# SBUF pools of a float32 decoder layer, regrouped by the engine that reads them: TensorE's operands at the low bytes of each partition, the rest at the high bytes

## The chip, the cores and the metric

The kernel runs on one core of a Trainium2 chip. The metric is the device time of one launch in microseconds; a run of the kernel is timed as a whole, and one further execution is profiled. TensorE (PE in the profile) multiplies, VectorE (DVE) and ScalarE (ACT) do everything elementwise, SyncE (SP) issues nearly all transfers from HBM into SBUF, the on-chip memory of 128 partitions. A tile takes the same bytes of every partition, so its place is one number: its first byte within a partition.

## The reference

One decoder layer over 256 tokens of width 2048, all in float32. What matters here is that nearly all of it is matrix products of the same 256 tokens with large weights, each weight used once:

```python
x = layer_norm(ALPHA * x + 0.5 * swiglu(x, ffn1_w_in[i], ffn1_w_out[i]), ...)   # D_FF = 5504
z = x @ mix_w_in[i]                                                              # 2048 x 11264
... short conv and gated linear recurrence on parts of z ...
merged = sigmoid(gate_conv) * (y_conv @ branch_w_conv[i]) + sigmoid(gate_hgrn) * (y_hgrn @ branch_w_hgrn[i])
x = layer_norm(ALPHA * x + merged @ mix_w_out[i], ...)
x = layer_norm(ALPHA * x + 0.5 * swiglu(x, ffn2_w_in[i], ffn2_w_out[i]), ...)
ple = sigmoid(x @ ple_w_gate[i]) * (p[i] @ ple_w_proj[i])
x = layer_norm(ALPHA * x + ple, ...)
```

## The kernel before

**Products.** Each float32 product is done as three float32r products (lines 733 to 735): weight and activation are each split into a rounded half and a remainder (`wh`, `wl` for the weight; `xh`, `xl`, or `gh`, `gl`, or `mh`, `ml`, or `ph`, `pl` for the activation), and `wh` times `xh`, `wl` times `xh`, `wh` times `xl` are accumulated into one PSUM tile `acc`. The activation half, 128 by 128, is the stationary operand that LDWEIGHTS loads (PEld in the profile); the weight half, 128 partitions by 512 columns (2,048 bytes of each partition), is the moving operand that MATMUL streams. So every MATMUL has a LDWEIGHTS of its own, and while one MATMUL streams its moving operand from SBUF, the LDWEIGHTS of the next reads its stationary operand from SBUF.

**Work.** A `Unit` is 256 tokens (two token tiles, t = 0 and 1) times a slab of a weight, at most 512 columns wide. A weight comes in pieces of two k-tiles: one DMA of 512 KB into a tile `raw` (four of them), one ScalarE cast to `wh` (line 679), one VectorE subtraction to `wl` (line 681), and then 2 k-tiles x 3 products for t = 0 and again for t = 1: 12 MATMULs for each piece. The units follow each other in phases: `ffn1`, `hgrn` (the projection `mix_w_in` with conv and recurrence in the background), `merge` (the gates and branch products, then `mix_w_out`), `ffn2`, `ple`.

**Where the halves lie.** `wh` and `wl` have six buffers each in the pool `wp` ("main"). The pool `region` is closed and opened again for every phase, with whatever tiles the phase needs, and what is free there holds some more `wh` and `wl` buffers: EXTRA says how many, and the plan deals the pieces out in that proportion, so in `ffn1` 4 of 10 pieces lie in the region, in `ffn2` 3 of 9, in `ple` 1 of 7, in `hgrn` and `merge` none:

```python
NMAIN = 6
EXTRA = {"ffn1": 4, "hgrn": 0, "merge": 0, "ffn2": 3, "ple": 1}
plan.append((u, ks, kind if (i + 1) * n // (NMAIN + n) > i * n // (NMAIN + n) else "main"))
```

The activation halves `xh`, `xl`, `gh`, `gl` lie in the pool `op`; in `merge`, half of the merged activation's halves (`mh`, `ml`, the last two of four column chunks) lie in the region; `ph` and `pl`, the stationary operands of the four products with `ple_w_proj`, lie among the constants.

**What orders the work.** The order within each engine comes from the program text and a scheduler; SBUF is filled by pools from one end, in the order in which they are opened: `const`, `res` (the residual `x`), `wp` (`raw`, `wh`, `wl`), `op`, `st` (small and intermediate tiles), and the region last. The built program uses nearly all of the 224 KiB of a partition.

Of the kernel before, what the change touches and what calls it, by code (L numbers as in the profile page):

```python
# [10 lines left out]
F32 = mybir.dt.float32  # L11
F32R = mybir.dt.float32r
# [5 lines left out]
P = 128  # L18
# [5 lines left out]
CC = 512  # L24
KG = 2
# [10 lines left out]


class Stat:
    """A stationary operand, transposed (contraction on partitions), as the two
    float32r halves of its float32 values; four k-tiles of one token tile per SBUF tile."""  # L40

    def __init__(self):
        self.parts = {}
# [4 lines left out]


class Unit:  # L50
    """256 tokens times a [nk * 128, width] slab of a weight."""

    def __init__(self, stat, w, row, nk, col, width, epi, split=SPLIT):
        self.stat, self.w, self.row, self.nk = stat, w, row, nk
# [11 lines left out]
def hybrid_layer(ctx: ExitStack, tc: tile.TileContext, x, p, ln_g, ln_b, ffn1_w_in, ffn1_w_out, mix_w_in,  # L66
# [4 lines left out]
    def pool(name, bufs=1, **kw):  # L71
        return ctx.enter_context(tc.tile_pool(name=name, bufs=bufs, **kw))

    const = pool("const")
    res = pool("res")
    wp = pool("wp")
    op = pool("op")
    st = pool("st")
    region = {}

    def open_region(kind):
        """The one SBUF region whose contents change from phase to phase."""
        if "ctx" in region:
            region.pop("ctx").close()
        region["ctx"] = ExitStack()
        region["kind"] = kind
        region["pool"] = region["ctx"].enter_context(tc.tile_pool(name=kind, bufs=1, reuse_waits="tile"))

    def rtile(shape, dtype=F32, **kw):
        return region["pool"].tile(shape, dtype, **kw)  # L90
# [2 lines left out]
    ps_t = pool("ps_t", 2, space=PSUM)  # L93
    ps_h = pool("ps_h", 2, space=PSUM)

    # ---------------------------------------------------------------- scheduling helpers
    state = {"tick": 0}
    later = []
    unsettled = set()
# [34 lines left out]
        return stat.get(t, k)  # L134

    def gated(part):
        """Queue the next instructions of a kind behind the one set down in gate."""
        ins, n = gate.get(part, (None, 0))
        gate[part] = (ins, n - 1)
        return tc.issue_after(ins) if n > 0 else nullcontext()  # L140

    def settle(c):
        """Force what is still to be done in place on column chunk c of x."""
        while c in unsettled:
            later.pop(0)[1]()

    # ---------------------------------------------------------------- constants, small inputs
    ident = const.tile([P, P], F32, name="ident")
    make_identity(nc, ident)
    ones = const.tile([P, 1], F32, name="ones")  # L150
    nc.gpsimd.memset(ones, 1.0)
    xt = [res.tile([P, D], F32, tag=f"x{t}", name=f"x{t}") for t in range(NT)]
    xin = x[0].rearrange("(t p) d -> t p d", p=P)
# [15 lines left out]
                                pattern=[[2 * b, n], [0, b]], channel_multiplier=-1)  # L169
        masks[b] = m  # L170

    # ---------------------------------------------------------------- operand transposition
    def transposed(src, nb):
        tp = ps_t.tile([P, CC], F32, tag="tp", name="tp")
        for i in range(nb):
# [1 line left out]
        return tp  # L177

    def halves(stat, t, g, src, nb, tag):
        """hi (rounded to float32r) and lo = src - hi (exact in float32r)."""  # L180
        where, bufs = (region["pool"], 4) if tag == "m" else (op, 8)
        h = where.tile([P, 4, P], F32R, tag=tag + "h", name=tag + "h", bufs=bufs)
        l = where.tile([P, 4, P], F32R, tag=tag + "l", name=tag + "l", bufs=bufs)
        hf = h[:, :nb, :].rearrange("p a b -> p (a b)")
        lf = l[:, :nb, :].rearrange("p a b -> p (a b)")
        nc.scalar.copy(hf, src)  # L186
        nc.vector.tensor_tensor(out=lf, in0=src, in1=hf.bitcast(F32), op=ALU.subtract)  # L187
        stat.parts[t, g] = (h, l)
# [3 lines left out]
        halves(stat, t, g, tp[:, : nb * P], nb, tag)  # L192

    def turn_blocks(dst, src, nb):
        """dst[:, a, :] = transpose of the a-th 128 columns of src, 32 by 32 on the vector engine."""
        cols = src[:, : nb * P].rearrange("p (a b c) -> p a b c", b=4, c=32)
        for q in range(4):
            for b in range(4):
                nc.vector.transpose(dst[32 * b : 32 * b + 32, :nb, 32 * q : 32 * q + 32], cols[32 * q : 32 * q + 32, :, b, :])  # L199
# [3 lines left out]
        turn_blocks(y, src, nb)  # L203
        halves(stat, t, g, y[:, :nb, :].rearrange("p a b -> p (a b)"), nb, tag)

    # ---------------------------------------------------------------- layer norm
    stats = {}

    def ln_stat(t, c):
# [2 lines left out]
        nc.vector.bn_stats(stats[t][:, c, :], xt[t][:, c * CC : (c + 1) * CC])  # L212

    def rsqrt_of(v, n, mul, add):
        """1 / sqrt(v * mul + add), one Newton step after the engines' sqrt and reciprocal."""
        w = st.tile([P, n], F32, tag=f"w{n}", name="w", bufs=4)
        m = st.tile([P, n], F32, tag=f"n{n}", name="m", bufs=4)
        r = st.tile([P, n], F32, tag=f"r{n}", name="r", bufs=4)
        u = st.tile([P, n], F32, tag=f"u{n}", name="u", bufs=4)
        nc.vector.tensor_scalar(out=w, in0=v, scalar1=4.0 * mul, scalar2=4.0 * add, op0=ALU.mult, op1=ALU.add)  # L220
        nc.scalar.activation(r, w, AF.Sqrt)
        nc.vector.tensor_scalar(out=m, in0=v, scalar1=-4.0 * mul, scalar2=-4.0 * add, op0=ALU.mult, op1=ALU.add)
        nc.vector.reciprocal(r, r)
        if n == 1:
            nc.vector.scalar_tensor_tensor(out=u, in0=r, scalar=m, in1=r, op0=ALU.mult, op1=ALU.mult)
        else:
            nc.vector.tensor_tensor(out=u, in0=r, in1=r, op=ALU.mult)
            nc.vector.tensor_tensor(out=u, in0=u, in1=m, op=ALU.mult)
        nc.vector.scalar_tensor_tensor(out=r, in0=u, scalar=3.0, in1=r, op0=ALU.add, op1=ALU.mult)
        return r  # L230

    def moments(t, scale):
        """Mean of x, and 1 / sqrt(variance + eps / scale^2)."""
        mv = st.tile([P, 2], F32, tag="mv", name="mv", bufs=2)
        nc.vector.bn_aggr(mv, stats[t])
        return mv[:, 0:1], rsqrt_of(mv[:, 1:2], 1, 1.0, LN_EPS / scale ** 2)

    def affine_rows(i, c, ts):
        """x = x * g + b for one column chunk, tokens on partitions."""
        gb = wp.tile([P, KG, CC], F32, tag="raw", name="gb", bufs=NRAW)  # L240
        for a, src in enumerate((ln_g, ln_b)):
            nc.sync.dma_start(gb[:, a, :], src[0, i : i + 1, c * CC : (c + 1) * CC].broadcast_to([P, CC]))

        def apply():
            for t in ts:
                xc = xt[t][:, c * CC : (c + 1) * CC]
                nc.vector.tensor_tensor(out=xc, in0=xc, in1=gb[:, 0, :], op=ALU.mult)
                nc.vector.tensor_tensor(out=xc, in0=xc, in1=gb[:, 1, :], op=ALU.add)
            unsettled.remove(c)

        defer(4, apply)

    def layer_norm(t, i, scale, stat):
        """x = LN(scale * x): at once as the next operand, behind it in place."""
        mean, r = moments(t, scale)

        def operand(c, xc):
            y = st.tile([P, CC], F32, tag="silu", name="y", bufs=2)
            tp = transposed(xc, 4)
            if t == 0 and c < 2:  # L260
                gate["pe"] = state["turned"], 1
            for a in range(4):
                k = i * 16 + 4 * c + a
                nc.scalar.activation(y[:, a * P : (a + 1) * P], tp[:, a * P : (a + 1) * P], AF.Identity,  # L264
                                     bias=gbT[:, 48 + k : 49 + k], scale=gbT[:, k : k + 1])
            halves(stat, t, c, y, 4, "x")

        for c in range(4):
            xc = xt[t][:, c * CC : (c + 1) * CC]
            norm = nc.vector.tensor_scalar(out=xc, in0=xc, scalar1=mean, scalar2=r, op0=ALU.subtract, op1=ALU.mult)  # L270
            defer((6 if t == 0 else 4) + c, lambda c=c, xc=xc: operand(c, xc))
            if c == 1 and t == 0:
                gate["lo"] = norm.ins, 2
        if t == NT - 1:
            for c in range(4):
                unsettled.add(c)
                defer(16 + 6 * c, lambda c=c: affine_rows(i, c, range(NT)))
# [6 lines left out]
            nc.vector.scalar_tensor_tensor(out=xc, in0=xc, scalar=r, in1=gb[4 + c], op0=ALU.mult, op1=ALU.add)  # L284
            nc.sync.dma_start(out[0, t * P : (t + 1) * P, c * CC : (c + 1) * CC], xc)

    # ---------------------------------------------------------------- the plan: units in order
    units = []

    def ffn(xs, w_in, w_out, ln_i, nxt):  # L290
# [38 lines left out]
    units.append(("ffn1", lambda: None))  # L329
    ffn(x0, w1i, w1o, 0, x1)  # L330

    # ---- mixer
    wm = mix_w_in[0]
    lb = const.tile([P, 8], F32, name="lb")
    oml = const.tile([P, 8], F32, name="oml")
# [2 lines left out]
    def small_loads():  # L338
# [10 lines left out]
        def place():  # L349
# [2 lines left out]
            nc.vector.tensor_copy(gbT, tp[:, :96])  # L352
            for t in range(NT):
                tp = transposed(pin[t], 2)
                ph = const.tile([P, 2, P], F32R, tag=f"ph{t}", name="ph")
                pl = const.tile([P, 2, P], F32R, tag=f"pl{t}", name="pl")
                hf = ph.rearrange("p a b -> p (a b)")
                nc.scalar.copy(hf, tp[:, :256])
                nc.vector.tensor_tensor(out=pl.rearrange("p a b -> p (a b)"), in0=tp[:, :256],
# [283 lines left out]
        units.append(Unit(x3, ple_w_gate[0], 0, 16, c * CC, CC, epi_s,  # L643
                          split=LATE if c == 3 else LONG if c == 0 else SPLIT))

    # ---------------------------------------------------------------- weight stream
    plan = []
    for u in units:
        if not isinstance(u, Unit):
# [10 lines left out]
    def weight_dma():  # L660
        i = cur["dma"]
        u, ks, _ = plan[i]
        raw = wp.tile([P, KG, CC], F32, tag="raw", name="raw", bufs=NRAW)
        r0 = u.row + ks[0] * P
        src = u.w[r0 : r0 + len(ks) * P, u.col : u.col + u.width].rearrange("(a p) c -> p a c", p=P)
        nc.sync.dma_start(raw[:, : len(ks), : u.width], src)
# [26 lines left out]
            else:  # L693
                return

    # ---------------------------------------------------------------- run
    region["kind"] = ""
    # The first loads are on their way: spin the tensor engine up to its full clock.
    warm = ps_h.tile([P, CC], F32, tag="hg", name="warm")
    for _ in range(6):  # L700
        nc.tensor.matmul(warm[:, :P], ident, ident, start=True, stop=True)
# [71 lines left out]
```

## Time and profile before

| | us |
|---|---|
| time of the three runs, median (lowest to highest) | 2303.39 (2301.42 to 2303.70) |
| profiled execution: span from first to last instruction | 2300.3 |
| PE busy in it | 2258.9 (98%) |
| PE weight loads (PEld) busy | 1856.6 (81%) |
| DVE busy | 1591.9 (69%) |
| ACT busy | 998.2 (43%) |

The profile gives no time of its execution beyond the span; the three runs lie 1.1 to 3.4 us above it. PE's busy time is the union of MATMULs whose modelled ends overlap the next one's start (a 512-column MATMUL is listed with about 0.39 us, and the next starts about 0.23 us after it), so 98% says that PE hardly ever waits, not that it is at its best rate. The rate shows in the starts.

### The profile page before, as it was taken

To read this page: it belongs to the slowest core of one execution; us is meant where nothing else is said; L and a number is where in the kernel's file an instruction comes from. 1 tells how busy PE (TensorE), PEld (TensorE's weight loads), DVE (VectorE), ACT (ScalarE), POOL (GpSimd) and SP (SyncE) were. 2 spreads that over 40 slices of the span, in tenths; PEclk is the share of its full clock that TensorE was granted. 3 is DMA by queue.
4 is the path that set the end of the run, shared out by engine and by line. 5 is a ranking of instruction groups with operands and counts; after the bars stand their busy time and mean duration, and the time that the engine had idled before them with its cause. 6 is when DMAs were issued, how large, how long until landed. Compare 5 with 4: busy or idle time off the path is not lost.

```text
span 2300.3 us, 27257 instructions
## 1 busy us (share of the span) xinstructions
PE 2258.9 (98%) x10074; PEld 1856.6 (81%) x10074; DVE 1591.9 (69%) x2534; ACT 998.2 (43%) x1160; POOL 10.6 (0%) x32
## 2 busy tenths in 40 slices
PE   9999999999999999899999999999999999999997
PEld 7888888888897788688788888778888888889886
DVE  6766466764685879978854875678755766567677
ACT  5443344434345443443444443634433444344463
POOL 1000000000000000000000000000000000000000
PEclk9999999999999999999999999999999999999999
DMA  8565555565564564454566555566555665555474
GB/s 281 183 207 193 186 184 192 178 212 186 160 203 132 165 201 147 164 191 131 174 196 198 181 197 190 171 201 227 188 192 180 197 197 185 192 192 175 161 236 152
DMA packets 225338, 430.01 MB, mean 187 GB/s; under 512 B 13741, under 2 KB 22453, under 8 KB 225205
## 3 DMA queue, kind: packets, MB, share of 16 engines
q1 hardware_dynamic: 225204, 428.27, 57.3%
q8 instruction: 79, 1.29, 0.2%
q14 instruction: 55, 0.44, 0.1%
HBM read 426.12 MB, written 2.10 MB: 186 GB/s over the span
## 4 chain that ended last, share of the span: by engine, by line
PE 82%; DVE 11%; DMA 3%; issue 2%; ACT 2%; DVEq 0%; SPq 0%; ACTq 0%
PE acc L733 27%; PE acc L735 27%; PE acc L734 27%; DVE wl L681 3%; DMA raw<-in_ple_w_gate_dram 1%; DMA raw<-in_ffn_w_in_dram 1%; PE gp L421 1%; DVE yT L199 1%; DVE uT L199 1%; DVE fT L199 1%; ACT wh L679 1%; DMA gb<-in_ln_g_dram 1%; ACT y L264 1%; DVE z L199 1%; DMA raw<-in_mix_w_in_dram 0%
## 5 line engine op out<-in xcount | busy, mean ns | idle before, releaser
L679 ACT CAST wh<-raw 128x1024 fp32r<-128x1024 f32 (+2 forms) x804 | 831.8, 1039 | 1085.1 <-PE acc L735 846.4
L681 DVE TENSOR_TENSOR wl<-raw,wh 128x1024 fp32r<-128x1024 f32 (+2 forms) x804 | 957.8, 1206 | 475.5 <-ACT wh L679 460.5
L733 PE MATMUL acc<-wh,xh 128*128 128x512 f32 (+1 forms) x2240 | 875.6, 393 | 8.2 <-ACT wh L679 3.8
L734 PE MATMUL acc<-wl,xh 128*128 128x512 f32 (+1 forms) x2240 | 871.9, 390 | 9.8 <-DVE wl L681 9.8
L735 PE MATMUL acc<-wh,xl 128*128 128x512 f32 (+1 forms) x2240 | 874.8, 391 | 1.3 <-DVE xl L187 1.0
L734 PEld LDWEIGHTS acc<-wl,xh 128*128 128x128 f32 x2240 | 423.6, 189 | 101.6 <-DVE wl L681 14.1
L733 PEld LDWEIGHTS acc<-wh,xh 128*128 128x128 f32 x2240 | 423.1, 189 | 96.0 <-ACT wh L679 5.5
L735 PEld LDWEIGHTS acc<-wh,xl 128*128 128x128 f32 x2240 | 423.0, 189 | 93.3 <-DVE xl L187 2.9
L733 PE MATMUL acc<-wh,gh 128*128 128x512 f32 x880 | 347.0, 394 | 2.9 <-ACT b L550 2.9
L735 PE MATMUL acc<-wh,gl 128*128 128x512 f32 x880 | 345.3, 392 | 0.0
L734 PE MATMUL acc<-wl,gh 128*128 128x512 f32 x880 | 343.2, 390 | 0.0
L199 DVE STREAM_TRANSPOSE hT<-h 32x128 f32<-32x128 f32 (+1 forms) x704 | 210.9, 300 | 9.8
L733 PEld LDWEIGHTS acc<-wh,gh 128*128 128x128 f32 x880 | 165.1, 188 | 38.8 <-ACT b L550 3.4
L735 PEld LDWEIGHTS acc<-wh,gl 128*128 128x128 f32 x880 | 165.1, 188 | 38.7
L734 PEld LDWEIGHTS acc<-wl,gh 128*128 128x128 f32 x880 | 165.3, 188 | 37.0
L306 DVE TENSOR_TENSOR h<-silu,acc 128x512 f32<-128x512 f32 (+1 forms) x44 | 29.5, 670 | 55.6 <-PE acc L735 55.5
L186 ACT CAST gh<-hT 128x512 fp32r<-128x512 f32 (+1 forms) x48 | 29.4, 613 | 57.4 <-DVE hT L199 57.4
L302 ACT ACTIVATE silu<-acc 128x512 f32<-128x512 f32 (+1 forms) x44 | 25.8, 585 | 56.2 <-PE acc L735 56.2
L319 DVE TENSOR_TENSOR x<-x,acc 128x512 f32<-128x512 f32 x32 | 21.8, 683 | 33.5 <-PE acc L735 33.5
L264 ACT ACTIVATE y<-tp,gbT 128x128 f32<-128x128 f32 x96 | 35.9, 465 | 7.8 <-PE tp L176 4.8
L187 DVE TENSOR_TENSOR gl<-hT,gh 128x512 fp32r<-128x512 f32 (+1 forms) x48 | 32.2, 672 | 0.0
L199 DVE STREAM_TRANSPOSE hT<-m 32x128 f32<-32x128 f32 x96 | 29.1, 303 | 1.4
(142 smaller groups left out, 726.1 us busy)
## 6 DMA issues: line engine op xcount, KB each, us to landing
raw<-in_ffn_w_in_dram SPq DMA_DIRECT2D x320, 512.0 KB, 4.7
raw<-in_mix_w_in_dram SPq DMA_DIRECT2D x176, 512.0 KB, 4.7
raw<-in_ffn_w_out_dram SPq DMA_DIRECT2D x168, 512.0 KB, 5.2
raw<-in_mix_w_out_dram SPq DMA_DIRECT2D x32, 512.0 KB, 4.8
raw<-in_ple_w_gate_dram SPq DMA_DIRECT2D x32, 512.0 KB, 5.4
raw<-in_ffn_w_in_dram SPq DMA_DIRECT2D x32, 384.0 KB, 4.0
raw<-in_branch_w_conv_dram SPq DMA_DIRECT2D x16, 512.0 KB, 5.0
raw<-in_branch_w_hgrn_dram SPq DMA_DIRECT2D x16, 512.0 KB, 4.6
```

The lines of the kernel that those rows point to most:

```text
L186: nc.scalar.copy(hf, src)
L187: nc.vector.tensor_tensor(out=lf, in0=src, in1=hf.bitcast(F32), op=ALU.subtract)
L199: nc.vector.transpose(dst[32 * b : 32 * b + 32, :nb, 32 * q : 32 * q + 32], cols[32 * q : 32 * q + 32, :, b, :])
L264: nc.scalar.activation(y[:, a * P : (a + 1) * P], tp[:, a * P : (a + 1) * P], AF.Identity, bias=gbT[:, 48 + k : 49 + k], scale=gbT[:, k : ...
L302: nc.scalar.activation(silu[t][:, :w], acc, AF.Silu)
L306: nc.vector.tensor_tensor(out=h[:, :w], in0=silu[t][:, :w], in1=acc, op=ALU.mult)
L421: nc.tensor.matmul(gp[:, (h * 2 + t) * 64 : (h * 2 + t + 1) * 64], kd[:, h, t * P : (t + 1) * P], qd[:, h, t, :], start=True, stop=True)
L679: nc.scalar.copy(h[:, :n, :w], raw[:, :n, :w])
L681: nc.vector.tensor_tensor(out=l[:, :n, :w], in0=raw[:, :n, :w], in1=h[:, :n, :w].bitcast(F32), op=ALU.subtract)
L733: nc.tensor.matmul(acc, sh, wh[:, a, : u.width], start=first, stop=False)
L734: nc.tensor.matmul(acc, sh, wl[:, a, : u.width], start=False, stop=False)
L735: nc.tensor.matmul(acc, sl, wh[:, a, : u.width], start=False, stop=last)
```

## The change

The pools are opened on two sides of the partition. From the low end: a new pool `low` (`ident`, `ones`, `ph`, `pl`), `wp` (now `wh`, `wl` alone), `op`, and the region. From the high end: `const` (what is left of it), `res`, a new pool `rp` (`raw`, and the row tiles `gb` that share its tag), `st`. No tile changes its size, its number of buffers or its tag; no line of computation is changed.

```diff
-    const = pool("const")
-    res = pool("res")
-    wp = pool("wp")
-    op = pool("op")
-    st = pool("st")
+    low = pool("low", side="left")
+    wp = pool("wp", side="left")
+    op = pool("op", side="left")
+    const = pool("const", side="right")
+    res = pool("res", side="right")
+    rp = pool("rp", side="right")
+    st = pool("st", side="right")
...
-        region["pool"] = region["ctx"].enter_context(tc.tile_pool(name=kind, bufs=1, reuse_waits="tile"))
+        region["pool"] = region["ctx"].enter_context(tc.tile_pool(name=kind, bufs=1, side="left", reuse_waits="tile"))
...
-    ident = const.tile([P, P], F32, name="ident")
+    ident = low.tile([P, P], F32, name="ident")
...
-    ones = const.tile([P, 1], F32, name="ones")
+    ones = low.tile([P, 1], F32, name="ones")
...
-        gb = wp.tile([P, KG, CC], F32, tag="raw", name="gb", bufs=NRAW)
+        gb = rp.tile([P, KG, CC], F32, tag="raw", name="gb", bufs=NRAW)
...
-                ph = const.tile([P, 2, P], F32R, tag=f"ph{t}", name="ph")
-                pl = const.tile([P, 2, P], F32R, tag=f"pl{t}", name="pl")
+                ph = low.tile([P, 2, P], F32R, tag=f"ph{t}", name="ph")
+                pl = low.tile([P, 2, P], F32R, tag=f"pl{t}", name="pl")
...
-        raw = wp.tile([P, KG, CC], F32, tag="raw", name="raw", bufs=NRAW)
+        raw = rp.tile([P, KG, CC], F32, tag="raw", name="raw", bufs=NRAW)
```

The rest of the diff takes out comments and docstrings. In the two built programs every engine has the same instructions in the same order, with the same waits between engines; what differs is the bytes that their operands name. The table gives them as built: first and last byte of the group in a partition, and the remainder of a tile's first byte by 512, the size of one stationary operand (within a row of the table all tiles and all operands begin a multiple of 512 bytes apart, so they share the remainder).

| tiles | read by PE as | bytes before | remainder | bytes after | remainder |
|---|---|---|---|---|---|
| `ident` | moving, in transposes | 16,512 to 17,023 | 128 | 16,512 to 17,023 | 128 |
| `ph`, `pl` | stationary | 20,416 to 24,511 | 448 | 17,056 to 21,151 | 160 |
| `x` | stationary, in transposes | 24,608 to 40,991 | 32 | 209,504 to 225,887 | 96 |
| `raw` | - | 40,992 to 57,375 | 32 | 193,120 to 209,503 | 96 |
| `wh`, main | moving | 57,376 to 81,951 | 32 | 21,152 to 45,727 | 160 |
| `wl`, main | moving | 81,952 to 106,527 | 32 | 45,728 to 70,303 | 160 |
| `xh`, `xl`, `gh`, `gl` | stationary | 106,528 to 172,063 | 32 | 70,304 to 135,839 | 160 |
| `wh`, `wl`, region | moving | 184,160 to 216,927 | 352 | 135,840 to 168,607 | 160 |
| `mh`, `ml` | stationary | 204,640 to 221,023 | 352 | 156,320 to 172,703 | 160 |

## Rows read from the trace of the kernel before

**Rows 1.** The page: span, busy time of the engines, and the granted TensorE clock in 40 equal slices of the span, in tenths of full speed (9 is 90% or more).

```profile
span 2300.3 us, 27257 instructions
PE 2258.9 (98%) x10074; PEld 1856.6 (81%) x10074; DVE 1591.9 (69%) x2534; ACT 998.2 (43%) x1160; POOL 10.6 (0%) x32
PEclk9999999999999999999999999999999999999999
```

**Rows 2.** The page: the chain of work that ended last, shares of the span by engine and by line.

```profile
PE 82%; DVE 11%; DMA 3%; issue 2%; ACT 2%; DVEq 0%; SPq 0%; ACTq 0%
PE acc L733 27%; PE acc L735 27%; PE acc L734 27%; DVE wl L681 3%; DMA raw<-in_ple_w_gate_dram 1%; DMA raw<-in_ffn_w_in_dram 1%; PE gp L421 1%; DVE yT L199 1%; DVE uT L199 1%; DVE fT L199 1%; ACT wh L679 1%; DMA gb<-in_ln_g_dram 1%; ACT y L264 1%; DVE z L199 1%; DMA raw<-in_mix_w_in_dram 0%
```

**Rows 3.** Busy time by stretch. Each stretch begins at the start of one MATMUL of line 733 and ends at the start of another, with nothing but MATMULs of lines 733 to 735, all 512 columns wide, between them; the one that began ahead of the stretch and still runs in it is counted, so one fewer began in it. In order: a stretch of `ffn1`, one of `merge` (gates and branch products), one of `merge` whose stationary operands are all `mh` and `ml`, one of `ffn2`. Columns: stretch, its length, busy us and count of each engine, granted clock, DMA share, GB/s.

```profile
core 0: us, PE busy (x) PEld busy (x) DVE busy (x) ACT busy (x) POOL busy (x), PEclk, DMA share, GB/s
278.77:456.06 177.29, 177.29 (x769) 144.15 (x768) 116.13 (x187) 74.43 (x78) 0.00 (x0) 1.00 0.58 190
1193.97:1357.17 163.20, 163.20 (x721) 135.13 (x720) 114.37 (x178) 71.57 (x76) 0.00 (x0) 1.00 0.60 193
1402.02:1413.22 11.20, 11.20 (x49) 9.02 (x48) 6.33 (x7) 4.21 (x4) 0.00 (x0) 1.00 0.57 190
1733.78:1910.92 177.14, 177.14 (x769) 144.13 (x768) 116.12 (x187) 74.47 (x78) 0.00 (x0) 1.00 0.58 190
```

**Rows 4.** Instructions in order of time, PE, `ple`: of MATMULs of line 733, every second one, so that six MATMULs lie between a row and the next. By the plan the six that begin at 2213.05 have their moving operands in the region, all others here in `wp`. Columns: start, duration, instruction.

```profile
2211.70 0.39 PE L733 MATMUL acc<-wh,xh 128*128 128x512 f32 x1
...
2213.05 0.40 PE L733 MATMUL acc<-wh,xh 128*128 128x512 f32 x1
...
2214.45 0.40 PE L733 MATMUL acc<-wh,xh 128*128 128x512 f32 x1
...
2215.83 0.62 PE L733 MATMUL acc<-wh,xh 128*128 128x512 f32 x2
...
2218.57 0.39 PE L733 MATMUL acc<-wh,xh 128*128 128x512 f32 x1
```

**Rows 5.** Instructions in order of time, PE, the first product with `ple_w_proj`: ten MATMULs begin between the first row and the last.

```profile
2183.57 0.39 PE L734 MATMUL acc<-wl,ph 128*128 128x512 f32 x1
2183.80 0.39 PE L735 MATMUL acc<-wh,pl 128*128 128x512 f32 x1
...
2185.67 0.39 PE L734 MATMUL acc<-wl,ph 128*128 128x512 f32 x1
2185.90 0.39 PE L735 MATMUL acc<-wh,pl 128*128 128x512 f32 x1
```

**Rows 6.** Instructions in order of time, PE, in `merge`, behind four transposes that interrupt the products: eleven MATMULs begin from the third row to the last (the last row not counted).

```profile
1376.71 0.60 PE L176 MATMUL tp<-ident,m 128*128 128x128 f32 x4
1377.06 0.48 PE L733 MATMUL acc<-wh,gh 128*128 128x512 f32 x1
1377.38 0.40 PE L734 MATMUL acc<-wl,gh 128*128 128x512 f32 x1
...
1379.69 0.39 PE L735 MATMUL acc<-wh,gl 128*128 128x512 f32 x1
1379.92 0.40 PE L733 MATMUL acc<-wh,mh 128*128 128x512 f32 x1
```

**Rows 7.** Groups of instructions by line and shape: count, busy us, mean ns of one, idle time of the engine before them and who ended it.

```profile
L681 DVE TENSOR_TENSOR wl<-raw,wh 128x1024 fp32r<-128x1024 f32 x764 | 923.2, 1222 | 456.9 <-ACT wh L679 442.1
L679 ACT CAST wh<-raw 128x1024 fp32r<-128x1024 f32 x764 | 800.5, 1052 | 1037.9 <-PE acc L735 805.3 <-DMA raw<-in_mix_w_in_dram 82.4 <-DMA raw<-in_ffn_w_in_dram 55.3
L733 PE MATMUL acc<-wh,mh 128*128 128x512 f32 x64 | 25.4, 397 | 0.0
L733 PE MATMUL acc<-wh,xh 128*128 128x384 f32 x128 | 43.0, 336 | 0.0
```

**Rows 8.** Who PE waited for, longest in total first: us in total, times, longest us.

```profile
PE acc L734 <- DVE wl L681: 9.8, 10, 3.0
PE acc L733 <- ACT b L550: 5.9, 2, 3.0
PE acc L733 <- ACT wh L679: 3.8, 3, 2.2
```

**Rows 9.** The page: DMA issues, KB each, median us from issue to landing.

```profile
raw<-in_ffn_w_in_dram SPq DMA_DIRECT2D x320, 512.0 KB, 4.7
```

## The prediction

> **What bounds the kernel now.** I read the page first. PE is busy 98% of the span, at the full granted clock in all 40 slices [rows 1], and its three product lines make 81% of the chain that ended last [rows 2]. The list of PE's waits is short: the longest sum, for `wl` from VectorE, is 9.8 us in ten waits [rows 8]. So the time is the number of products times the distance from one start to the next, and what is to be read is that distance. The listed durations of about 0.39 us are no help, since they overlap. I therefore took stretches that begin and end on a product's start, hold nothing but 512-column products, and have no stall.
>
> They do not run at one rate [rows 3]. In `ffn1`, 177.29 us / 768 = 230.85 ns a product. In `ffn2`, 177.14 / 768 = 230.65 ns. In the gates and branches of `merge`, 163.20 / 720 = 226.67 ns. Where `mh` and `ml` are stationary, 11.20 / 48 = 233.3 ns. The granted clock is 1.00 in all four, the DMA moves 190 to 193 GB/s, and VectorE is busy 65 to 70% of three of them and 57% of the slowest; so neither the clock nor the other engines' load goes with the rate. What does is where the operands lie. The fast stretch has all of them in `wp` and `op`. In `ffn1` 4 of 10 moving pairs lie in the region, in `ffn2` 3 of 9. In the slowest stretch the moving operands are all in `wp`, and the stationary ones in the region.
>
> The order of time in `ple` shows it product by product [rows 4]. Six products from `wp` take 2213.05 - 2211.70 = 1.35 us (225 ns each, to the rounding of the rows); the six from the region take 1.40, the six after them, from `wp` again, 1.38, and the next twelve 2.74 together, where twelve at 226.67 ns would take 2.72. So one pass over a region pair costs some 0.07 to 0.08 us, half of it paid by products behind it whose operands are in the right place. That also tells why `ffn1` and `ffn2` are slow throughout: there the next region pair comes before the stream has recovered.
>
> A stationary tile in a third place is slow too: `ph` and `pl`, near byte 20,000, give (2185.90 - 2183.57) / 10 = 233 ns [rows 5]. After a break in the stream the same slow rate appears for about ten products with all operands in `wp` and `op`: (1379.92 - 1377.38) / 11 = 231 ns [rows 6].
>
> **What I take from this.** Slow places are one above byte 184,000 and one near 20,000; the places between 57,000 and 172,000 give 226.67 ns. "Far from the low end" alone does not fit, since `ph` is at the low end. What fits all three with one cause is the remainder of an operand's first byte by 512: it is 32 for all of `wp` and `op`, 352 for the region (the small tiles of `st` lie before it and shift it), 448 for `ph` and `pl`. (By 512 and no more, since in the fast stretch stationary operands begin 0, 512, 1,024 and 1,536 bytes into their tiles.) Fast is the case in which both operands that PE reads at the same time have one remainder. After the change `ph` and `pl`, `wp`, `op` and the region follow each other on the low side without `st` between them, and the remainder is 160 in all of them. By this reading every product gets 226.67 ns. The reading "high bytes are slow", under which `ph` is an exception, gives the same: region tiles come down to at most byte 172,703, about where `gl` ends today.
>
> **The change part by part.**
> - `ffn1`: 2,952 products of 512 columns (16 units of 16 k-tiles, less the two 384-column units, plus the output units: 3,144 in all, 192 of them narrow). 2,952 x (230.85 - 226.67) = 12.3 us [rows 3].
> - `ffn2`: 2,952 x (230.65 - 226.67) = 11.7 us [rows 3].
> - `merge`: `mh` and `ml` are stationary in 64 x 3 = 192 products [rows 7]: 192 x (233.3 - 226.67) = 1.3 us [rows 3].
> - `ple`: 36 pieces, 1 in 7 in the region, so 5 pieces, each passed over twice: 10 x 0.08 = 0.8 us [rows 4]. `ph`, `pl`: 16 x 3 = 48 products x (233 - 226.67) = 0.3 us [rows 5].
> - The 384 narrow products: not seen apart from region pairs, so the price is bounded by nothing and by the whole 4.2 ns each, 1.6 us. I take nothing, since at a narrower operand the overlap of the two reads is different.
> - To be taken off: the slow products behind a break stay, for no break goes away. Each costs 11 x (231 - 226.67) = 0.05 us [rows 6], and what the two FFN phases have of them is counted above as gain. The narrow margin of PE's waits [rows 8] suggests a dozen such breaks in each: -1.0 us at most, and as some lie in the transposes of `merge`, where nothing was counted, I take -0.8.
> - ScalarE's cast (1,052 ns) and VectorE's subtraction (1,222 ns) now read `raw` and write `wh`, `wl` at other bytes; the residual `x` and the small tiles move too. Whether their durations change no row can tell. A piece keeps PE for 12 x 226.67 = 2,720 ns, so each has over half of it free [rows 7]; at nothing or at 2% more (25 ns) they stay hidden. Without that cover 2% of the subtractions would be 764 x 0.024 = 18 us. The loads: 512 KB per 2.72 us is 193 GB/s, what the fast stretch already moves [rows 3]; a load lands in 4.7 us [rows 9] and four `raw` tiles are in turn, so there is room.
> - Transposes read `x` as stationary against `ident`, at remainders 32 and 128 now, 96 and 128 then; 32 groups of four, 0.35 us each [rows 6]. At the 3% between the fast and slow rates that is 0.3 us to either side; I take nothing.
> - No instruction, wait or transfer is added, removed or moved, so no queue has something new in it.
>
> Sum: 12.3 + 11.7 + 1.3 + 0.8 + 0.3 - 0.8 = 25.6 us. The span goes from 2300.3 to 2274.7. The median of the runs lies 3.1 us over the span, and I keep that: 2303.4 - 25.6 = 2277.8 us, 1.1% less. With the narrow products at their bound and no deduction it is 2275; with the unknown DVE and ACT prices reaching the 11% of the chain that is VectorE's [rows 2] at 1% (2.5 us), 2281. The likeliest case's own range is 2274 to 2282.
>
> **The rivals.**
> - *Nothing happens* (0.07). Place in a partition is no cause, and the rates differ by something that goes with the phases, or by which operand lies below the other: the region's moving tiles lie above their stationary ones before and after alike. For it: no instruction changes. Against: `merge` has both rates within 30 us, with the same engines at work [rows 3], and `mh` lies above its moving tiles, not below. It gives 2303.4. The Trainium skill ("SBUF — State Buffer", section "Who interferes with whom") speaks for this rival: TensorE and ScalarE never wait on anyone, the one contention is on the port pair that VectorE and GpSimd share, and no section makes a tile's byte matter. By that rule the sum would be nil; the trace does not agree, with 226.67 and 233.3 ns at the same clock.
> - *Slower* (0.11): the low end itself is slow. `ph` near byte 20,000 is the only thing PE reads there, and it is slow [rows 5]. `wh` now goes to bytes 21,152 to 45,727, where no row of today lies (the lowest byte seen at the full rate is 57,376). If the slow place reaches up over them, two of three products everywhere read from it, and as one slow operand holds back its neighbours [rows 4], all run at about 233.3 ns: the two FFN phases lose 5,904 x 2.5 = 15 us, the 2,500 products of `hgrn` and `merge` that are fast today 2,500 x 6.6 = 17 us: 2335 us. It decides if the slow place ends above byte 30,000 or so. Against it: remainders explain `ph` without it.
> - *Half the gain* (0.06): what costs is the jump between `wp` and the region, about 100,000 bytes before and after. Then only `mh`, `ml`, `ph`, `pl` gain and the FFN phases keep most of their loss: 2290 to 2301. Against it: the slowest stretch has no such jump in its moving operands [rows 3].
> - *More* (0.05): 226.67 ns itself holds some loss, and remainder 160 takes that away. 512 columns at the full 2.4 GHz are 213.3 ns, so 13.3 ns of each product are something else. With half of it gone, 9,200 products x 6.7 = 61 us more, 2216; with 1 to 2 ns, 2260 to 2269. Nothing in the trace shows a stretch under 226.67.
>
> **How the numbers follow.** Likeliest (0.71): 2277.8. A change under 0.2% (4.6 us) can't be told from none. Faster: 0.71 + 0.06 + 0.05, less a little of the half gain that falls under 0.2%: 0.81. Same: 0.08. Slower: 0.11. The range leaves out the slower case, most of "more", and about half of "nothing": 2270 to 2304 holds about 0.82.
>
> **What would show it.** Right: stretches of `ffn1` and `ffn2` at 226.7 ns a product (768 products in 174.1 us), the `mh` stretch at 226.7, a region pair in `ple` that leaves no trace, and `ph` at 227; PE's waits and the 226.67 ns stretch of `merge` unchanged. High bytes as the cause, not remainders: the same, but `ph` still at 233. Wrong: the fast stretch of `merge` over 226.7 (low end slow, or remainder 160 bad as such), or `ffn1` still at 230.85 (place is no cause). The prediction also fails if the gain is there and VectorE's or ScalarE's waits grow by as much.

## The result and the profile after

The changed kernel takes 2279.49 us (median of four runs, 2277.24 to 2280.95) beside 2302.68 us for the kernel before in the same comparison: a ratio of 0.9898, 95% interval 0.9884 to 0.9912. Forecast were 2277.8 us and a range of 2270 to 2304. The span of its profiled execution is 2277.6 us, 22.7 less than before; the sum of the prediction had 25.6 less.

The same four kinds of stretch as in [rows 3], taken between the same products of the program: a stretch of `ffn1`, one of `merge`, the one with `mh` and `ml` stationary, one of `ffn2`. Columns as there; 768, 720, 48 and 768 products begin in them.

```profile
core 0: us, PE busy (x) PEld busy (x) DVE busy (x) ACT busy (x) POOL busy (x), PEclk, DMA share, GB/s
274.44:448.52 174.08, 174.08 (x770) 144.21 (x768) 116.07 (x187) 74.41 (x78) 0.00 (x0) 1.00 0.60 193
1181.69:1344.89 163.20, 163.20 (x722) 135.22 (x720) 114.38 (x178) 71.44 (x76) 0.00 (x0) 1.00 0.60 193
1389.37:1400.25 10.88, 10.88 (x50) 9.01 (x48) 6.28 (x7) 4.21 (x4) 0.00 (x0) 1.00 0.60 190
1716.00:1890.08 174.08, 174.08 (x769) 144.27 (x768) 116.07 (x187) 74.41 (x78) 0.00 (x0) 1.00 0.60 193
```

Divide each length by its products: 226.67 ns in all four. `ffn1` was at 230.85, `ffn2` at 230.65, the `mh` stretch at 233.3; the stretch of `merge` that was at 226.67 has kept its 163.20 us to the last digit. The granted clock is 1.00 in both kernels, and the other engines' busy time in the stretches has not moved by more than 0.2 us.

PE's order of time in `ple`, the products of line 736 (line 733 before) around a pair in the region, which begins at 2200.00. The rows are three products apart:

```profile
2198.64 0.39 PE L736 MATMUL acc<-wh,xh 128*128 128x512 f32 x1
2199.32 0.39 PE L736 MATMUL acc<-wh,xh 128*128 128x512 f32 x1
2200.00 0.39 PE L736 MATMUL acc<-wh,xh 128*128 128x512 f32 x1
2200.68 0.39 PE L736 MATMUL acc<-wh,xh 128*128 128x512 f32 x1
2201.36 0.39 PE L736 MATMUL acc<-wh,xh 128*128 128x512 f32 x1
```

Every distance is 0.68 us: the region pair leaves no trace, where it and the six products behind it took 1.40 and 1.38 us in place of 1.36 [rows 4]. And `ph`, `pl`, in a part without a break:

```profile
2163.99 0.39 PE L738 MATMUL acc<-wh,pl 128*128 128x512 f32 x1
...
2166.03 0.39 PE L738 MATMUL acc<-wh,pl 128*128 128x512 f32 x1
```

Nine distances in 2.04 us are 226.7 ns each; [rows 5] had 233. `ph` lies at bytes 17,056 and up now, lower than before, and `wh` right behind it, so the low end is not a bad place.

### The profile page after: what moved, and what is told of

The parts are those of the page before. It is cut to its first block, busy times and chain, and to the rows that moved or that the text cites. A ratio compares the mean times of both kernels' runs of the same rounds, so it can differ in the third digit from the quotient of the medians.

```text
span 2277.6 us, 27257 instructions
## 1 busy us (share of the span) xinstructions
PE 2232.2 (98%) x10074; PEld 1856.1 (81%) x10074; DVE 1591.9 (70%) x2534; ACT 996.6 (44%) x1160; POOL 10.5 (0%) x32
## 4 chain that ended last, share of the span: by engine, by line
PE 82%; DVE 11%; DMA 3%; issue 2%; ACT 1%; SPq 0%; DVEq 0%; ACTq 0%
PE acc L737 27%; PE acc L738 27%; PE acc L736 27%; DVE wl L684 3%; DMA gb<-in_ln_g_dram 1%; PE gp L424 1%; DVE yT L202 1%; DVE uT L202 1%; DVE fT L202 1%; DMA raw<-in_ple_w_gate_dram 1%; DMA raw<-in_ffn_w_in_dram 1%; DMA raw<-in_mix_w_in_dram 1%; DVE z L202 1%; ACT y L267 1%; ACT wh L682 0%
## 5 line engine op out<-in xcount | busy, mean ns | idle before, releaser
L737 PE MATMUL acc<-wl,xh 128*128 128x512 f32 (+1 forms) x2240 | 869.5, 389 | 11.1 <-DVE wl L684 11.1
```

Of the source, the lines that this page charges most:

```text
L737: nc.tensor.matmul(acc, sh, wl[:, a, : u.width], start=False, stop=False)
```

## The experiments

Three theories were to be told apart. **Remainder**: the two operands that PE reads, moving and stationary, must begin at the same byte modulo some size (the prediction had taken 512). **High bytes**: what lies high in the partition is read more slowly. **Jump**: changing between two far places costs. e1, e4 and e5 keep the program's instructions, their order and their waits; e2, e3 and e6 differ from the changed kernel in some waits, and in the order of some of ScalarE's instructions in one layer norm, since a tile of the region comes free at another time. All are profiled, and those with an interval are timed against the kernel before, which had a median of 2300.67 us beside e1 to e4 and 2300.63 us beside the rest.

**e1: everything in line, at the high end.** The kernel before, with `st` opened ahead of `wp`; so nothing with odd sizes stands between `wp`, `op` and the region. The region stays at bytes 184,160 and up.

```diff
+    st = pool("st")
     wp = pool("wp")
     op = pool("op")
-    st = pool("st")
```

> The kernel before with one edit: the pool of small tiles (st) is opened ahead of wp, so that wp, op and the region follow each other. All moving and stationary halves but ph and pl then have one remainder by 512 (352); the region stays at bytes 184,160 and up, and everything else lies at most 12,096 bytes higher than before. Theory 'remainder' (both operands that PE reads at a time need the same remainder by 512): ffn1 and ffn2 run at 226.7 ns a product, the mh stretch too, ph (448 against 352) stays at 233; time 2278 to 2282 us. Theory 'high bytes are slow': nothing changes, ffn1 230.85 ns, time 2302 to 2304 us. Theory 'jump between wp and region': nothing changes either.

Measured: 2280.21 us, ratio 0.9914 (0.9897 to 0.9930). The four stretches:

```profile
273.86:447.94 174.08, 174.08 (x770) 144.15 (x769) 116.06 (x187) 74.66 (x78) 0.00 (x0) 1.00 0.59 193
1180.55:1343.74 163.19, 163.19 (x721) 135.13 (x720) 114.35 (x178) 71.39 (x75) 0.00 (x0) 1.00 0.59 192
1388.22:1399.10 10.88, 10.88 (x49) 9.01 (x48) 6.28 (x7) 4.22 (x4) 0.00 (x0) 1.00 0.58 193
1715.08:1889.16 174.08, 174.08 (x769) 144.14 (x768) 116.04 (x187) 74.67 (x78) 0.00 (x0) 1.00 0.59 193
```

All at 226.67 ns, with the region exactly where it was, 184,160 to 216,927, and with the jump from `wp` to it only 12,096 bytes narrower, of some 126,800. That ends both rivals. The one operand that does not agree in this kernel, `ph` and `pl` (448 against 352, 96 bytes apart), is still at the other rate: nine distances in 2.11 us, 234 ns. They are the same nine products that took 2.04 us in the changed kernel.

```profile
2163.09 0.40 PE L735 MATMUL acc<-wh,pl 128*128 128x512 f32 x1
...
2165.20 0.40 PE L735 MATMUL acc<-wh,pl 128*128 128x512 f32 x1
```

**e4: stationary operands 64 bytes off.** The changed kernel with 64 unused bytes between `wp` and `op`.

```diff
     wp = pool("wp", side="left")
+    gap = pool("gap", side="left")
     op = pool("op", side="left")
...
+    gap.tile([P, 16], F32, name="gap")
```

> The changed kernel with 64 unused bytes between wp and op: xh, xl, gh, gl and the region lie 64 bytes off the remainder of wh and wl in wp, while the region agrees with op. Theory 'remainder': the stretch of merge that ran at 226.67 ns in both kernels slows to 229 to 233.3 ns, as all its products now have unlike operands; ffn1 and ffn2 slow too, in the six of ten pairs that lie in wp; time 2300 to 2340 us. 'High bytes are slow' and 'jump': nothing changes against the changed kernel, 2278 to 2281 us.

Measured: 2320.12 us, ratio 1.0086 (1.0071 to 1.0101): 64 bytes that nobody uses make the kernel slower than it was before the change.

```profile
279.41:457.51 178.10, 178.10 (x769) 143.87 (x768) 116.15 (x187) 74.35 (x78) 0.00 (x0) 1.00 0.58 189
1199.50:1367.50 168.00, 168.00 (x722) 134.64 (x720) 114.62 (x178) 71.45 (x76) 0.00 (x0) 1.00 0.58 189
1413.18:1424.38 11.20, 11.20 (x50) 9.02 (x49) 6.29 (x7) 4.19 (x4) 0.00 (x0) 1.00 0.57 186
1746.94:1925.20 178.26, 178.26 (x769) 143.82 (x768) 116.19 (x187) 74.34 (x78) 0.00 (x0) 1.00 0.58 189
```

The stretch of `merge` that held 226.67 ns in every other kernel is at 168.00 us / 720 = 233.33 ns. `ffn1` (231.90) and `ffn2` (232.11) are less slow than that, since here the region's pairs are the ones that agree with `op`, and more slow than before, since now the majority of pairs is off. In all these stretches `wh` and `wl` agree with each other; it is the moving operand against the stationary one that counts.

**e2, e3, e6: how many bytes.** The changed kernel with an unused tile at the front of the region, of a different size in `ffn1` and `ffn2`; one run gives two offsets.

```diff
+PAD = {"ffn1": 64, "ffn2": 32}          # e3: 128, 256; e6: 192, 224
...
+        if kind in PAD:
+            region["pool"].tile([P, PAD[kind] // 4], F32, tag="pad", name="pad")
```

> The changed kernel with an unused tile at the front of the region: 64 bytes in ffn1, 32 bytes in ffn2. Region tiles then lie 64 (ffn1) or 32 (ffn2) bytes off the remainder of wp and op; merge, hgrn and ple are as in the changed kernel. Theory 'remainder', with 512 or anything above 64 as what counts: ffn1 back to about 230.8 ns a product and ffn2 to about 230.6, time about 2302 us. With only the remainder by 64 counting: ffn1 at 226.7, ffn2 at 230.6, time about 2291. With only 32 counting, or with 'high bytes are slow': both at 226.7, time 2278 to 2281.

> As the run before, with 128 bytes in ffn1 and 256 in ffn2. Theory 'remainder': if it counts by 512, both phases are at about 230.7 ns a product and the time is about 2302 us; if by 256, ffn1 at 230.8 and ffn2 at 226.7, about 2291; if by 128, both at 226.7, 2278 to 2281. 'High bytes are slow': both at 226.7, 2278 to 2281.

> As e2 and e3, with 192 unused bytes ahead of the region's tiles in ffn1 and 224 in ffn2. Theory 'remainder by 256': both are off, so both phases run at 229 to 231 ns a product, time 2295 to 2302 us. Rival 'some offsets are as good as none': one phase or both at 226.7, 2278 to 2291 us.

Measured, one run each: 2300.10, 2285.88 and 2298.85 us. The stretches of `ffn1` and `ffn2` (768 products each), in this order of the kernels:

```profile
278.06:455.35 177.29, 177.29 (x769) 144.16 (x768) 116.14 (x187) 74.37 (x78) 0.00 (x0) 1.00 0.59 190
1731.59:1908.42 176.83, 176.83 (x769) 144.16 (x768) 116.08 (x187) 74.36 (x78) 0.00 (x0) 1.00 0.58 190
```

```profile
277.20:453.67 176.47, 176.47 (x770) 144.15 (x768) 116.18 (x187) 74.42 (x78) 0.00 (x0) 1.00 0.59 191
1723.39:1897.47 174.08, 174.08 (x770) 144.19 (x768) 116.07 (x187) 74.44 (x78) 0.00 (x0) 1.00 0.59 193
```

```profile
278.03:455.15 177.12, 177.12 (x769) 143.97 (x768) 116.17 (x187) 74.41 (x78) 0.00 (x0) 1.00 0.58 190
1730.20:1906.97 176.77, 176.77 (x769) 144.20 (x768) 116.08 (x187) 74.38 (x78) 0.00 (x0) 1.00 0.58 190
```

In ns a product, for the offset of the region's moving operands against `op`:

| offset in bytes, moving less stationary | `ffn1` (4 of 10 pairs off) | `ffn2` (3 of 9 pairs off) |
|---|---|---|
| 0 (changed kernel) | 226.67 | 226.67 |
| 32 | | 230.25 |
| 64 | 230.85 | |
| 128 | 229.78 | |
| 192 | 230.63 | |
| 224 | | 230.17 |
| 256 | | 226.67 |
| 320 (kernel before) | 230.85 | 230.65 |

So what counts is the remainder by 256, not by 512 as the prediction had it: 256 bytes are as good as none, and the kernel before, 320 off, runs `ffn1` at the very 230.85 ns that 64 gives. Of the multiples of 32 bytes that were tried (the pools place tiles by 32), none but 0 and 256 is free; 128 costs about three quarters of what 64 does. An offset of 160 by this count is that of `ph` and `pl` in e1; 96 has no stretch of its own.

**e5 and a second run of the changed kernel: does the byte itself count?** In e5 the changed kernel gets 96 unused bytes at its low end, which puts every operand of the products at a multiple of 256.

```diff
+    low.tile([P, 24], F32, name="gap")
     ident = low.tile([P, P], F32, name="ident")
```

> The changed kernel with 96 unused bytes at its low end, so that all moving and stationary halves of the products begin at a multiple of 256 bytes (they had the remainder 160 by 256 in the changed kernel, 96 in e1, 32 in wp and op before). Theory 'only the two operands against each other': 226.67 ns a product everywhere, as in the changed kernel, 2277 to 2281 us. Rival 'the absolute byte counts as well': a product that begins at a multiple of 256 touches 8 pieces of 256 bytes instead of 9; any gain shows as a stretch under 226.67 ns, and 1 ns is worth 9.2 us.

> The changed kernel once more beside e5, to see what differs from one execution to the next: the FFN phases at 226.8 ns a product as in its first profile, and the phase ple, from the first product with ple_w_proj to the last one, between 103 and 107 us where the first profile had 105.9 and the kernel before 103.4. If ple's length is set by the layer norm and the loads around it and not by the products' rate, it stays there although its products are faster. Time 2277 to 2281 us.

Measured: e5 2277.41 us, ratio 0.9899 (0.9879 to 0.9920); the changed kernel again 2278.32 us, ratio 0.9898 (0.9883 to 0.9913). The stretches of `ffn1` and `merge` in e5:

```profile
275.77:449.85 174.08, 174.08 (x769) 144.19 (x768) 116.08 (x187) 74.45 (x78) 0.00 (x0) 1.00 0.59 193
1182.58:1345.78 163.20, 163.20 (x722) 135.13 (x720) 114.38 (x178) 71.21 (x75) 0.00 (x0) 1.00 0.59 193
```

226.67 ns again. With a common remainder by 256 of 32 (`wp` and `op` before), 160 (after), 96 (e1) and 0 (e5) the rate is the same; of the remainders that ran, only the difference counts. Nothing here beats the changed kernel.

## Why the prediction was right, point by point

**What bounds the kernel**: as told. PE is 98% busy in both kernels, and its rate moved where its operands moved.

**`ffn1` and `ffn2`** were to give 12.3 and 11.7 us, less 0.8 for what stays slow behind breaks: 23.2. From the first product of the phase to the first of the next, `ffn1` went from 724.11 to 712.58 us and `ffn2` from 723.54 to 712.09: 11.5 and 11.45, together 23.0, the narrow products' 0.3 in it.

**`mh` and `ml`** were to give 1.3: `merge` from its first `mh` product on went from 79.80 to 78.45 us, 1.35. `hgrn` and the rest of `merge`, where nothing was expected, gave 0.8 (648.34 to 647.51 us), which is within what this length differs by from run to run (647.07 to 648.50 us in the runs where its products are at 226.67 ns).

**Narrow products**: bounded by 0 and 1.6 us and taken as 0. Their distance fell from 174.17 to 173.47 ns on the mean, over 384 products 0.3 us.

**`ple` is the term that was mis-sized.** With `ph` and `pl` it was to give 1.1 us. From its first product with `ple_w_proj` to the last product of the kernel it took 103.42 us before and 105.88 after: 2.5 longer, 3.6 off the working. That is more than the whole difference between 25.6 and 22.7; the 0.8 of `hgrn` and `merge` goes the other way. Its products did get faster, but by less than the working has: over those whose next product starts within 0.3 us (412 before, 409 after) the mean distance fell from 229.0 to 227.5 ns, 0.6 us in all. The rest is mostly what the working had at nothing, the waits of PE. Who PE waited for in `ple`, in the kernel before (2183 to 2287), after (2158 to 2264.1) and after again (2159 to 2264); columns as in [rows 8]:

```profile
PE acc L734 <- DVE wl L681: 0.6, 1, 0.6
```

```profile
PE acc L737 <- DVE wl L684: 2.1, 2, 1.2
PE acc L736 <- ACT pp L625: 1.3, 2, 0.8
```

```profile
PE acc L736 <- ACT pp L625: 2.2, 2, 1.3
```

PE now waits 3.4 us (2.2 in the second execution) where it waited 0.6: for ScalarE's copy `pp`, which frees a PSUM tile, and for `wl`. Behind both stand loads. The copy has its turn on ScalarE behind the cast of the next weight piece, and that cast stands idle for its load (in brackets, us and what ended them), before and after:

```profile
2188.95 1.05 ACT L679 CAST wh<-raw 128x1024 fp32r<-128x1024 f32 x1 [0.50 <-DMA raw<-in_ple_w_gate_dram]
2189.90 0.58 ACT L622 COPY pp<-acc 128x512 f32<-128x512 f32 x1
```

```profile
2165.33 1.05 ACT L682 CAST wh<-raw 128x1024 fp32r<-128x1024 f32 x1 [2.04 <-DMA raw<-in_ple_w_gate_dram]
2166.28 0.58 ACT L625 COPY pp<-acc 128x512 f32<-128x512 f32 x1
```

Some 6 us ahead of each `wl` that PE waited for after the change, VectorE stands idle for the layer norm's rows `gb`; the same places before and after:

```profile
2239.82 1.29 DVE L247 TENSOR_TENSOR x<-x,gb 128x512 f32<-128x512 f32 x2 [1.80 <-DMA gb<-in_ln_g_dram]
2251.55 1.29 DVE L247 TENSOR_TENSOR x<-x,gb 128x512 f32<-128x512 f32 x2 [2.38 <-DMA gb<-in_ln_g_dram]
```

```profile
2217.15 1.29 DVE L250 TENSOR_TENSOR x<-x,gb 128x512 f32<-128x512 f32 x2 [2.97 <-DMA gb<-in_ln_g_dram]
2229.00 1.29 DVE L250 TENSOR_TENSOR x<-x,gb 128x512 f32<-128x512 f32 x2 [2.62 <-DMA gb<-in_ln_g_dram]
```

That these idle times and PE's waits belong together is read from the order on ScalarE and VectorE; no run here changes a load alone. Over all nine profiles the idle time of that cast runs from 0.50 to 3.11 us, and PE's wait for `pp` rises with it, from 0.1 us or less to 2.2. It does not follow the products' rate: in e4, with its gate products at 233 ns, the cast is idle for 2.78 us and `ple` takes 105.65 us; in e5, with them at 226.67, 1.16 and 102.99. So the step that was off is that `ple` was priced as products times distance; what the products gained there is smaller than what its loads differ by from one execution to the next. Of the kernel before there is one profile, with the shortest of these waits; why its load came so early, and whether it would again, no run shows.

**The other costs taken as nothing** hold: the cast went from 1,052 to 1,050 ns and the subtraction from 1,222 to 1,223 [rows 7]; PE's longest sum of waits, for `wl`, from 9.8 to 11.1 us [rows 8].

```profile
L684 DVE TENSOR_TENSOR wl<-raw,wh 128x1024 fp32r<-128x1024 f32 x764 | 924.0, 1223 | 440.9 <-ACT wh L682 407.8
L682 ACT CAST wh<-raw 128x1024 fp32r<-128x1024 f32 x764 | 799.4, 1050 | 1017.2 <-PE acc L738 770.9 <-DMA raw<-in_mix_w_in_dram 70.5 <-DMA raw<-in_ffn_w_in_dram 60.6
```

**The rivals.** That place is no cause fell with every run: 64 unused bytes are worth some 40 us between the changed kernel and e4. That the low end is slow fell with `ph` at 226.7 ns at byte 17,056 and `wh` behind it. The jump fell with e1. The "more" case, that 226.67 ns holds a loss which another remainder takes away, fell for the four common remainders that ran.

**The title of the change is not its cause.** Low and high have no part in it: e1 leaves the region at the high end, moves `wp` and `op` up, and has the same gain. What the regrouping did was to take the small tiles of `st` from between `op` and the region, and two small constants, 96 bytes in all, from between `ph` and `wp`.

**Weak places of the working that did no harm.** The change makes the operands agree by 512 and so by 256 as well, and its result alone could not have told the two periods apart. [rows 5] lies within ten products of a break, where operands that agree also start 231 ns apart [rows 6]; that `ph` itself was slow is shown by e1 beside the changed kernel, not by that row. The count of 2,952 products is right, but comes from 22 units of 16 k-tiles, not 16.

## What to carry to other kernels

Where TensorE streams back to back with a weight load for each product, look at the distance of starts, in stretches without a stall, before believing that a busy engine is at its best: two rates at one clock were the sign here. Then compare the first bytes of the moving and the stationary tiles modulo 256; pools that hold odd-sized tiles belong behind, not between, those that hold matmul operands, as e1 shows with one line moved. The runs show this for float32r products with 512 columns and a weight load each; other types and shapes were not tried, but for the 384 columns here. A faster product does not shorten a stretch that waits for loads, so count the gain only where PE has no waits.

## What the runs showed of the hardware that was not expected

- Float32r products of 128 by 128 by 512 start 226.67 ns apart at the full granted clock if both operands begin at the same byte modulo 256, at each of the four common remainders that ran and at bytes from 17,056 to 221,023 of the partition. They start 233.3 ns apart where every stationary operand has a remainder 64 bytes above its moving one (e4; 320 bytes above in the `mh` stretch before). The prediction had a period of 512 bytes; it is 256.
- An operand that is off also slows the products behind it, as a break in the stream does [rows 4, 6]: read product by product, ten of them at the offset of the kernel before (64 by the remainder), three to seven at the other offsets. So 4 of 10 pairs off cost 4.2 ns in every product of `ffn1`, and six of ten (e4) only 5.2.
- Which two reads meet, a product's moving operand with its own stationary one or with that of the next, whose load begins while it streams, no run here tells apart. Why the period is 256 bytes is open too.
